# Offsets inside the weight buffers of the 512-column products, and a head written in a fixed order

## The chip, the cores and the metric

One core of a Trainium2 chip runs the program. TensorE (PE) multiplies matrices, VectorE (DVE), ScalarE (ACT) and GpSimd (POOL) work on elements, and SyncE (SP) and POOL issue transfers between the chip's memory and SBUF. The metric is the time of one execution on the device, in microseconds; the median of several runs counts.

## The reference, cut to what matters

One layer of an encoder on x (256 tokens of 2048 numbers, float32), with 16 learned tokens (`meta`) put in front, so T = 272.

```python
n      = rms_norm(h, norm_mix)                 # h: 272 x 2048
p      = n @ w_in                              # 14*512 mixing columns and 4*2048 gate columns
z      = [rglru(...), hyena(...), retention(...), hgrn2(...)]     # four mixers, each 272 x 512
up     = einsum('btnw,nwd->btnd', z, w_branch_out)
merged = sum over n of sigmoid(gate_cols) * up
h      = h + merged @ w_out
n      = rms_norm(h, norm_ffn)
h      = h + (silu(n @ w_gate) * (n @ w_up)) @ w_down             # 5632 hidden columns
out    = rms_norm(h, norm_final)               # the 256 tokens without meta
```

## The kernel before, in words

All weights come through one queue (SP) in pieces of 512 KB, `raw`, 128 partitions of 1024 numbers, in four buffers (`piece`). Each piece is split into two parts that TensorE multiplies in its fp32r format: `hi`, a cast (ACT, L112), and `lo` = raw − hi (DVE, L113). The first `NPOOL` = 2 pieces are split on POOL (L110, L113). `hi` and `lo` have three buffers each, of 1024 + `WPAD` = 1088 numbers, 4352 bytes, a multiple of 256; `piece` has a parameter `skip`, the number of elements by which the piece lies further in its buffer. The activations are split in the same way, and a product is three matmuls: hi by hi, lo by hi, hi by lo.

There are two kinds of product. In `mix_chunk` (L312 to L314) the weights are the stationary operand, 128 by 128, and the normalized tokens `nh`, `nl` move past: 272 columns (first token `t0` = 0), 258 (14) or 256 (16), each k of them a row of 320 numbers with 48 free ones (`LEAD`) in front. Here `skip` is 16 where `t0` isn't 0. In `xs_gemm` (L134 to L136) it is the other way round: tokens are stationary, and 512 columns of weights move past. It is used for the gates (stationary `nh`, 1536 matmuls), the up product of the mixers (`zh`, 384), the output product (`mth`, 384), the gate and up products of the feed-forward (`n2h`, 1056 each), and its down product in two parts (`hidh`, 576 and 480). Here `skip` isn't given and is 0. The last 120 matmuls of the down product take weights from separate buffers, `held`.

The head of the program loads `par` (constants), `xm` (meta tokens) and two tiles of 128 tokens of x, in halves of 512 KB. POOL issues `mlp` and `rope` before it does anything else. Each tile's squares are summed on ACT (L244) and DVE (L246) by quarters, a reciprocal root is made (L248, L161 to L163), and the tile is scaled by quarters on ACT (L255) and DVE (L257). Then, for each of 16 k, TensorE transposes 128 by 128 of both tiles (L280, `ptn`), ACT writes `nh` (L281) and DVE `nl` (L282). A scheduler decides the order on each engine; pieces are given a priority 250 steps ahead, and `SCHED` lists the order in which the mixers ask for chunks. Late in the mixing stage, `mixer_d` makes heads in `po` (L679 to L681), normalizes them in `head_out` into `on` (squares L499, root L161 to L163, scaling L509), transposes them (L512, `pt`) and multiplies them into `zz`; its gates are sigmoids `sg` (L520) and `fb` (L551), `bm` (L570) belongs to the decay.

## Time and profile before

| what | value |
|---|---|
| median of 3 runs | 1707.37 us (1707.24 to 1707.54) |
| the profiled execution's own time | 1708.65 us |
| its span, first to last instruction | 1706.9 us |
| TensorE busy | 1667.4 us, 98% |
| weight loads of TensorE | 1437.0 us, 84% |
| DVE, ACT, POOL busy | 954.6, 803.8, 80.6 us |
| mean granted clock of TensorE | 0.996 of full speed |
| moved by DMA | 313.81 MB, mean 184 GB/s |

Busy time is the time in which an engine executes instructions; weight loads run beside matmuls. A clock of 0.996 is a mean: 1.00 stands for 2.4 GHz and 0.50 for 1.2 GHz. The duration that the trace gives for one matmul includes a modelled end and is longer than the distance to the next, so lengths of matmuls are read from the distances of their starts.

### The profile page before, as it was taken

What the parts mean: (1) busy time and instruction counts of PE and PEld (TensorE: products, weight loads), DVE (VectorE), ACT (ScalarE), POOL (GpSimd) and SP (SyncE); (2) the same over time, 40 slices, a digit from 0 to 9 for tenths busy, and PEclk for the clock granted to TensorE, in tenths of its full rate; (3) what the DMA queues carried; (4) which work ended last, traced back from release to release, by engine and by line L of the source; (5) the groups of instructions that cost most, each with busy time, mean ns of one, the idle gap of its engine ahead of it and who ended that gap; (6) DMA issues with size and microseconds to landing.
All of it is one profiled execution on the core that took longest, in us unless ns stands there. A gap on an engine that the chain in (4) does not pass through costs nothing.

```text
span 1706.9 us, 22379 instructions
## 1 busy us (share of the span) xinstructions
PE 1667.4 (98%) x8844; PEld 1437.0 (84%) x8844; DVE 954.6 (56%) x1140; ACT 803.8 (47%) x969; POOL 80.6 (5%) x74
## 2 busy tenths in 40 slices
PE   6999999999999999999999999999999999999997
PEld 5999999989978888888888888888888888888886
DVE  6755895486675445454455545454545444544554
ACT  5544465474574444444445544444444334444443
POOL 2000000001002002010020000000000000000001
PEclk9999999999999999999999999999999999999999
DMA  6546444546356555555666555555555555555554
GB/s 238 184 140 193 144 140 145 181 139 212 111 172 211 188 194 186 196 194 188 197 198 210 197 197 186 192 190 187 191 190 188 194 196 190 194 185 190 193 191 142
DMA packets 87225, 313.81 MB, mean 184 GB/s; under 512 B 9824, under 2 KB 10112, under 8 KB 86992
## 3 DMA queue, kind: packets, MB, share of 16 engines
q1 hardware_dynamic: 84960, 304.42, 54.0%
q0 software_dynamic: 2160, 7.97, 1.5%
q8 instruction: 69, 1.13, 0.3%
q14 instruction: 36, 0.29, 0.1%
HBM read 309.17 MB, written 2.10 MB: 182 GB/s over the span
## 4 chain that ended last, share of the span: by engine, by line
PE 93%; DVE 4%; ACT 2%; issue 1%; DMA 0%; SPq 0%; ACTq 0%
PE acc L135 23%; PE acc L136 23%; PE acc L134 23%; PE mix L312 5%; PE mix L314 5%; PE mix L313 5%; DVE lo L113 1%; PE pth L948 1%; PE last L1006 1%; PE last L1005 1%; PE last L1007 1%; DMA x<-in_x_dram 0%; ACT hi L112 0%; PE pl L635 0%; PE pg L801 0%
## 5 line engine op out<-in xcount | busy, mean ns | idle before, releaser
L113 DVE TENSOR_TENSOR lo<-raw,hi 128x1024 fp32r<-128x1024 f32 x556 | 686.5, 1235 | 668.9 <-ACT hi L112 668.6
L112 ACT CAST hi<-raw 128x1024 fp32r<-128x1024 f32 x556 | 585.0, 1053 | 759.9 <-PE acc L136 620.1
L136 PE MATMUL acc<-hi,n2l 128*128 128x512 f32 x704 | 274.0, 389 | 0.0
L135 PE MATMUL acc<-lo,n2h 128*128 128x512 f32 x704 | 273.9, 389 | 0.0
L312 PE MATMUL mix<-nh,hi 128*128 128x272 f32 (+2 forms) x896 | 255.0, 287 | 3.4 <-DVE cg L521 1.8
L314 PE MATMUL mix<-nh,lo 128*128 128x272 f32 (+2 forms) x896 | 252.8, 287 | 4.3 <-DVE lo L113 4.3
L313 PE MATMUL mix<-nl,hi 128*128 128x272 f32 (+2 forms) x896 | 255.9, 287 | 0.0
L134 PE MATMUL acc<-hi,n2h 128*128 128x512 f32 x704 | 249.4, 390 | 0.0
L135 PE MATMUL acc<-lo,nh 128*128 128x512 f32 x512 | 200.1, 391 | 2.8 <-DVE lo L113 2.8
L136 PE MATMUL acc<-hi,nl 128*128 128x512 f32 x512 | 199.8, 390 | 0.0
L134 PE MATMUL acc<-hi,nh 128*128 128x512 f32 x512 | 181.7, 391 | 0.6 <-ACT hi L112 0.6
L312 PEld LDWEIGHTS mix<-nh,hi 128*128 128x128 f32 x896 | 169.9, 190 | 5.9 <-issue 2.8
L314 PEld LDWEIGHTS mix<-nh,lo 128*128 128x128 f32 x896 | 168.6, 190 | 6.1 <-DVE lo L113 5.2
L313 PEld LDWEIGHTS mix<-nl,hi 128*128 128x128 f32 x896 | 170.2, 190 | 0.7 <-issue 0.2
L136 PEld LDWEIGHTS acc<-hi,n2l 128*128 128x128 f32 x704 | 132.1, 188 | 27.5
L134 PEld LDWEIGHTS acc<-hi,n2h 128*128 128x128 f32 x704 | 132.2, 188 | 27.1
L135 PEld LDWEIGHTS acc<-lo,n2h 128*128 128x128 f32 x704 | 132.2, 188 | 27.1
L136 PE MATMUL acc<-hi,hidl 128*128 128x512 f32 x312 | 121.4, 389 | 0.0
L135 PE MATMUL acc<-lo,hidh 128*128 128x512 f32 x312 | 121.4, 389 | 0.0
L135 PEld LDWEIGHTS acc<-lo,nh 128*128 128x128 f32 x512 | 96.1, 188 | 24.0 <-DVE lo L113 4.5
L134 PEld LDWEIGHTS acc<-hi,nh 128*128 128x128 f32 x512 | 96.0, 188 | 20.9 <-ACT hi L112 1.3
L136 PEld LDWEIGHTS acc<-hi,nl 128*128 128x128 f32 x512 | 96.2, 188 | 19.6
(388 smaller groups left out, 1644.7 us busy)
## 6 DMA issues: line engine op xcount, KB each, us to landing
raw<-in_w_dram SPq DMA_DIRECT2D x568, 512.0 KB, 3.3
x<-in_x_dram SPq DMA_DIRECT2D x4, 512.0 KB, 8.7
h<-in_x_dram SPq DMA_DIRECT2D x8, 256.0 KB, 4.2
out_dram<-h SPq DMA_DIRECT2D x8, 256.0 KB, 3.1
lruw<-in_lruw_dram POOLq DMA_DIRECT2D x2, 512.0 KB, 6.3
dm<-in_decay_dram POOLq DMA_DIRECT2D x4, 256.0 KB, 4.3
nf<-in_norm_final_dram POOLq DMA_DIRECT2D x1, 1024.0 KB, 6.6
rot<-ck POOLq DMA_DIRECT2D x2, 272.0 KB, 6.0
```

What stands on the lines that cost most here:

```text
L112: A.copy(hi, raw)
L113: ins = (G if i < NPOOL else V).tensor_tensor(lo, raw, hi.bitcast(F32), op=SUB)
L134: PE.matmul(acc[t], xh[:, k, s], wh[:, j], start=(i + j == 0), stop=False)
L135: PE.matmul(acc[t], xh[:, k, s], wl[:, j], start=False, stop=False)
L136: PE.matmul(acc[t], xl[:, k, s], wh[:, j], start=False, stop=(i + j == n - 1))
L312: PE.matmul(o, wh[:, j, s], nh[:, k, t0:T], start=(k == 0), stop=False)
L313: PE.matmul(o, wh[:, j, s], nl[:, k, t0:T], start=False, stop=False)
L314: PE.matmul(o, wl[:, j, s], nh[:, k, t0:T], start=False, stop=(k == KT - 1))
L948: PE.transpose(pt[:, j * P:j * P + P], s[:, j * P:j * P + P], ident)
L1005: PE.matmul(acc, xh, wh, start=(k == 0), stop=False)
L1006: PE.matmul(acc, xh, wl, start=False, stop=False)
L1007: PE.matmul(acc, xl, wh, start=False, stop=(k == 2 * n - 1))
```

## The change

`xs_gemm` gets a parameter `skip` and hands it to `piece`. Every call gives a value of its own: gate 16 elements (64 bytes), up 4 (16 bytes), output 32 (128), feed-forward gate 48 (192), feed-forward up 56 (224), down 24 and 8 (96 and 32). The head is written in a fixed order: `par` comes in two transfers, the second behind x; `mlp` and `rope` are issued later on POOL; 40 transposes of `ident` (`pwarm`) are put ahead of those of x; the squares of both tiles come first, with one reciprocal root for both; then the scaling goes by quarters, tile 0 on ACT and tile 1 on DVE, between the steps over k; POOL splits its two pieces by quarters; and the first three pieces of ACT and DVE are held behind `nh` and `nl` of k = 5, 9 and 13.

```diff
--- before.py
+++ after.py
@@ -31,6 +31,7 @@
 NPOOL = 2
+NWARM = 40
@@ -83,13 +84,21 @@
         return psp.tile(list(shape), F32, tag="ps", name=name)
     par = const.tile([P, NPAR], F32, name="par")
-    nc.sync.dma_start(par, a["par"])
+    nc.sync.dma_start(par[:, :PCOL["norm_ffn"]], a["par"][:, :PCOL["norm_ffn"]])
     def pc(name, i=0, rows=P):
         return par[:rows, PCOL[name] + i:PCOL[name] + i + 1]
     ident = const.tile([P, P], F32, name="ident")
     make_identity(nc, ident)
+
+    last = {}
+    behind = {}
+
+    def after(ins, prev):
+
+        tc.add_manual_dep(ins.ins, prev.ins.name, mybir.DependencyInfo(
+            mybir.DependencyClass.NoSync, mybir.DependencyReason.DATA), reason="order at the head")
     wpos = [0]
     first = []
@@ -107,17 +116,26 @@
                 hi, lo = [p.tile([P, 1024 + WPAD], F32R, tag=x, name=x)[:, skip:skip + 1024]
                           .rearrange("p (k n) -> p k n", k=kt) for p, x in ((hip, "hi"), (lop, "lo"))]
             if i < NPOOL:
-                G.tensor_scalar(hi, raw, 1.0, 0.0, op0=MUL, op1=ADD)
+                for j in range(kt):
+                    ins = G.tensor_scalar(hi[:, j], raw[:, j], 1.0, 0.0, op0=MUL, op1=ADD)
+                    if "G" in last:
+                        after(ins, last["G"])
+                    ins = G.tensor_tensor(lo[:, j], raw[:, j], hi[:, j].bitcast(F32), op=SUB)
+                    last["G"] = ins
             else:
-                A.copy(hi, raw)
-            ins = (G if i < NPOOL else V).tensor_tensor(lo, raw, hi.bitcast(F32), op=SUB)
+                ins = A.copy(hi, raw)
+                if i in behind:
+                    after(ins, behind[i][0])
+                ins = V.tensor_tensor(lo, raw, hi.bitcast(F32), op=SUB)
+                if i in behind:
+                    after(ins, behind[i][1])
             if i == 1:
                 first.append(ins.ins)
         return hi, lo
     later = []
-    def xs_gemm(xh, xl, kts, at=2):
+    def xs_gemm(xh, xl, kts, at=2, skip=0):
 
         acc = [accp.tile([P, 512], F32, tag="acc", name=f"acc{t}") for t in range(2)]
@@ -126,7 +144,7 @@
             if i == at:
                 while later:
                     later.pop(0)()
-            wh, wl = piece(2, 512)
+            wh, wl = piece(2, 512, skip=skip)
             for j in range(2):
                 k = kts[i + j]
                 for t in range(2):
@@ -193,7 +211,6 @@
 
     mlp = H("mlp", 128 + T, rows=64)
-    G.dma_start(mlp, a["mlp"])
     f2 = mc.tile([P, T], F32, name="f2")
     def sine(dst, src, bias):
@@ -208,6 +225,7 @@
         A.activation(dst, x, AF.Sin)
     def sines():
+        G.dma_start(mlp, a["mlp"])
         p1 = ps("pf1")
         PE.matmul(p1[:64, :T], mlp[:33, 0:64], mlp[:33, 128:], start=True, stop=True)
         f1 = TT("f1", T, rows=64)
@@ -230,42 +248,20 @@
         for i in range(2):
             nc.sync.dma_start(halves[i], a["x"][t * P:t * P + P, i * 1024:i * 1024 + 1024])
         xts.append(halves)
+    nc.sync.dma_start(par[:, PCOL["norm_ffn"]:], a["par"][:, PCOL["norm_ffn"]:])
     ss = tiny("ss", 3, 4)
     rs = tiny("rs", 3)
     def quarter(g, q):
         return xts[g][q // 2][:, q % 2 * 512:q % 2 * 512 + 512]
...
     dump = H("dump", 256)
     A.activation(dump, xm, AF.Square, accum_out=ss[:, 2, 0:1])
     pm = ps("pmeta")
     PE.matmul(pm[:, 0:1], par[:, PCOL["ind"]:PCOL["ind"] + P], ss[:, 2, 0:1], start=True, stop=True)
     rsqrt(rs[:, 2:3], pm[:, 0:1], 1.0 / D)
-    squares(0, "AVAV")
-    squares(1, "AVAV")
     V.tensor_scalar(xm, xm, rs[:, 2:3], None, op0=MUL)
-    rescale(0, "AVAV")
-    rescale(1, "VAVA")
     pm = ps("pmeta")
     for b in range(2):
         PE.transpose(pm[:, b * P:b * P + P], xm[:, b * P:b * P + P], ident)
@@ -273,7 +269,41 @@
     gain = par[:, PCOL["norm_mix"]:PCOL["norm_mix"] + KT].rearrange("p (k b) -> p k b", b=2)
     V.tensor_tensor(nm, pm[:, 0:256].rearrange("p (b t k) -> p k b t", b=2, k=8),
                     gain[:, :, :, None].to_broadcast([P, 8, 2, META]), op=MUL)
-    split(nh[:, :, 0:META], nl[:, :, 0:META], nm.rearrange("p k b t -> p (k b) t"))
+    nm = nm.rearrange("p k b t -> p (k b) t")
+    last["A"] = A.copy(nh[:, :, 0:META], nm)
+    last["V"] = V.tensor_sub(nl[:, :, 0:META], nm, nh[:, :, 0:META].bitcast(F32))
+
+
+    pw_ = ps("pwarm")
+    for i in range(NWARM):
+        PE.transpose(pw_[:, i % 4 * P:i % 4 * P + P], ident, ident)
+
+
+    for t in range(2):
+        for q, e in enumerate("AVAV"):
+            dump = H("dump", 512)
+            x, acc = quarter(t, q), ss[:, t, q:q + 1]
+            if e == "A":
+                ins = A.activation(dump, x, AF.Square, accum_out=acc)
+            else:
+                ins = V.scalar_tensor_tensor(dump, x, 1.0, x, op0=MUL, op1=MUL, accum_out=acc)
+            after(ins, last[e])
+            last[e] = ins
+    V.tensor_reduce(rs[:, 0:2], ss[:, 0:2], op=ADD, axis=mybir.AxisListType.X)
+    rsqrt(rs[:, 0:2], rs[:, 0:2], 1.0 / D)
+
+
+    def rescale(q):
+        for t in range(2):
+            x, r = quarter(t, q), rs[:, t:t + 1]
+            if t == 0:
+                ins = A.activation(x, x, AF.Copy, scale=r)
+            else:
+                ins = V.tensor_scalar(x, x, r, None, op0=MUL)
+            after(ins, last["AV"[t]])
+            last["AV"[t]] = ins
+
+    rescale(0)
     for k in range(KT):
         pt = ps("ptn")
         for t in range(2):
@@ -281,6 +311,13 @@
         anchor = [A.activation(nh[:, k, META:], pt[:, :SEQ], AF.Copy, scale=pc("norm_mix", k)),
                   V.scalar_tensor_tensor(nl[:, k, META:], pt[:, :SEQ], pc("norm_mix", k), nh[:, k, META:].bitcast(F32),
                                          op0=MUL, op1=SUB)]
+        for e, ins in zip("AV", anchor):
+            after(ins, last[e])
+            last[e] = ins
+        if k % 4 == 1:
+            if k < 12:
+                rescale(k // 4 + 1)
+            behind[NPOOL + k // 4 - 1] = anchor
     def late(eng, ins):
         tc.add_manual_dep(ins.ins, anchor[eng].ins.name, mybir.DependencyInfo(
@@ -685,7 +722,8 @@
     def mixer_c():
         rope = H("rope", 2, T)
-        G.dma_start(rope, a["rope"])
+        with tc.issue_after(first[0]):
+            G.dma_start(rope, a["rope"])
         def rotate(x, n):
             y = S("rot", NW, n)
@@ -840,7 +878,7 @@
     nsh, nsl = nh[:, :, META:], nl[:, :, META:]
     def gate(d, b, first=False):
-        acc = xs_gemm(nsh, nsl, range(KT))
+        acc = xs_gemm(nsh, nsl, range(KT), skip=16)
         for t in range(2):
             s = half("sig")
             lut(s, acc[t], AF.Sigmoid, new=first and t == 0)
@@ -868,7 +906,7 @@
     def up(d):
         mg = [mgp.tile([P, 512], F32, tag="mg", name="mg") for _ in range(2)]
         for i, b in enumerate(BORDER):
-            acc = xs_gemm(zh[b], zl[b], range(NW))
+            acc = xs_gemm(zh[b], zl[b], range(NW), skip=4)
             for t in range(2):
                 s = sigs.pop((d, b, t))
                 if i == 0:
@@ -908,7 +946,7 @@
         rsqrt(rstd[:, i], rstd[:, i], 1.0 / D)
     for d in range(4):
-        acc = xs_gemm(mth, mtl, range(KT))
+        acc = xs_gemm(mth, mtl, range(KT), skip=32)
         for t in range(2):
             h = half("h")
             hh[t, d] = h
@@ -939,8 +977,8 @@
     hidl = [hid_p.tile([P, 4 * n, SEQ], F32R, tag=f"hid{i}l", name=f"hidl{i}") for i, n in enumerate(GU_HALF)]
     def gate_up(part, c):
-        ag = xs_gemm(n2h, n2l, range(KT), at=4)
-        au = xs_gemm(n2h, n2l, range(KT))
+        ag = xs_gemm(n2h, n2l, range(KT), at=4, skip=48)
+        au = xs_gemm(n2h, n2l, range(KT), skip=56)
         def turn(t, s):
             pt = ps("pth")
@@ -963,7 +1001,7 @@
     def down(part, ds):
         for d in ds:
-            acc = xs_gemm(hidh[part], hidl[part], range(4 * GU_HALF[part]))
+            acc = xs_gemm(hidh[part], hidl[part], range(4 * GU_HALF[part]), skip=8 if part else 24)
             for t in range(2):
                 add(acc[t], t, d, part == 1)
 
```

On POOL, at the head: the pieces of the two first weights, and the transfers `mlp`, `rope`. Before:

```order
L196 DMA mlp<-in_mlp_dram 64x400
L688 DMA rope<-in_rope_dram 128x544
masks.py:199 ISA
masks.py:199 AFFINE_SELECT ident<-ident 128x128
L110 TENSOR_SCALAR hi<-raw 128x1024
L113 TENSOR_TENSOR lo<-raw,hi 128x1024
```

After:

```order
masks.py:199 AFFINE_SELECT ident<-ident 128x128
L120 TENSOR_SCALAR hi<-raw 128x256
L123 TENSOR_TENSOR lo<-raw,hi 128x256
L120 TENSOR_SCALAR hi<-raw 128x256
...
L123 TENSOR_TENSOR lo<-raw,hi 128x256
L228 DMA mlp<-in_mlp_dram 64x400
L236 MEMSET f_98 64x272
L418 DMA trow<-in_trow_dram 128x31
L726 DMA rope<-in_rope_dram 128x544
```

The two transfers moved behind eight pairs of quarter pieces. On TensorE at the head (`x_0_...` are the first halves of the two token tiles, `mix_...` the two PSUM banks of the first chunk), before:

```order
L271 MATMUL pmeta<-ident,xm 128x128 x2
L280 MATMUL ptn<-ident,x_0_105 128x128 x4
L280 MATMUL ptn<-ident,x_0_109 128x128 x4
L312 MATMUL mix_261<-nh,hi 128x272
L312 MATMUL mix_262<-nh,hi 128x272
L280 MATMUL ptn<-ident,x_0_105 128x128
L280 MATMUL ptn<-ident,x_0_109 128x128
```

After:

```order
L267 MATMUL pmeta<-ident,xm 128x128 x2
L279 MATMUL pwarm<-ident 128x128 x40
L310 MATMUL ptn<-ident,x_0_104 128x128
L310 MATMUL ptn<-ident,x_0_108 128x128
...
L349 MATMUL mix_298<-nh,hi 128x272
L349 MATMUL mix_299<-nh,hi 128x272
L350 MATMUL mix_298<-nl,hi 128x272
L351 MATMUL mix_298<-nh,lo 128x272
L350 MATMUL mix_299<-nl,hi 128x272
```

The four transposes of either tile stood together and now alternate, behind the new ones. On ACT at the end of the first `mixer_d`, before:

```order
L499 ACTIVATE on_2564,ssh<-po 128x128 x4
L112 CAST hi<-raw 128x1024
L570 ACT_TABLE_LOAD
L570 ACTIVATE bm<-ff 128x32
L162 ACT_TABLE_LOAD
L162 ACTIVATE rsh<-rsh 128x4
L520 ACT_TABLE_LOAD
L520 ACTIVATE sg<-mix_2973 128x256
L112 CAST hi<-raw 128x1024
L520 ACTIVATE sg<-mix_2974 128x256
L551 ACTIVATE fb<-mix_2846 128x256
L551 ACTIVATE fb<-mix_2847 128x256
```

After:

```order
L536 ACTIVATE on_2614,ssh<-po 128x128 x4
L607 ACT_TABLE_LOAD
L607 ACTIVATE bm<-ff 128x32
L180 ACT_TABLE_LOAD
L180 ACTIVATE rsh<-rsh 128x4
L126 CAST hi<-raw 128x1024 x2
L588 ACT_TABLE_LOAD
L588 ACTIVATE fb<-mix_2896 128x256
L588 ACTIVATE fb<-mix_2897 128x256
L174 CAST zh_286<-zz 128x512
L557 ACTIVATE sg<-mix_3023 128x256
```

One `hi` stood ahead of the root (L162, after the change L180) and now stands behind it, and `fb` stood behind two `sg` and now comes ahead of them. On TensorE at the same place, before, where 34 mixing matmuls stand between the last `po` and `pt`:

```order
L314 MATMUL mix_2973<-nh,lo 128x256
L312 MATMUL mix_2974<-nh,hi 128x256
L313 MATMUL mix_2974<-nl,hi 128x256
L314 MATMUL mix_2974<-nh,lo 128x256
L512 MATMUL pt<-ident,on_2564 128x128 x4
L312 MATMUL mix_3102<-nh,hi 128x272
L313 MATMUL mix_3102<-nl,hi 128x272
L314 MATMUL mix_3102<-nh,lo 128x272
L312 MATMUL mix_3102<-nh,hi 128x272
```

After, where 40 stand between the last `po` and the first `pt`:

```order
L349 MATMUL mix_3024<-nh,hi 128x256
L350 MATMUL mix_3024<-nl,hi 128x256
L549 MATMUL pt<-ident,on_2614 128x128
L351 MATMUL mix_3024<-nh,lo 128x256
L349 MATMUL mix_3023<-nh,hi 128x256
L549 MATMUL pt<-ident,on_2614 128x128
L350 MATMUL mix_3023<-nl,hi 128x256
L549 MATMUL pt<-ident,on_2614 128x128
L351 MATMUL mix_3023<-nh,lo 128x256
L349 MATMUL mix_3024<-nh,hi 128x256
L549 MATMUL pt<-ident,on_2614 128x128
L350 MATMUL mix_3024<-nl,hi 128x256
```

The four `pt` stood together behind the last matmul of their chunk and now stand among its matmuls; 20 more of that chunk follow the last of them.

## Rows read from the trace of the kernel before

**Rows 1.** The page: busy us, share of the span, instructions.

```profile
PE 1667.4 (98%) x8844; PEld 1437.0 (84%) x8844; DVE 954.6 (56%) x1140; ACT 803.8 (47%) x969; POOL 80.6 (5%) x74
```

**Rows 2.** TensorE's waits, the longest group: us in total, times, longest.

```profile
PE pmeta L271 <- DVE xm L266: 4.7, 1, 4.7
```

**Rows 3.** Timeline, 512-column products: start, duration, ... (first and last of 179 matmuls).

```profile
1349.65 0.39 PE L135 MATMUL acc<-lo,hidh 128*128 128x512 f32 x1
...
1390.00 0.39 PE L135 MATMUL acc<-lo,hidh 128*128 128x512 f32 x1
```

**Rows 4.** Timeline, mixing: pairs of first and last, 95, 191 and 96 matmuls.

```profile
108.61 0.29 PE L312 MATMUL mix<-nh,hi 128*128 128x272 f32 x1
...
120.21 0.28 PE L313 MATMUL mix<-nl,hi 128*128 128x272 f32 x1
...
120.46 0.28 PE L312 MATMUL mix<-nh,hi 128*128 128x256 f32 x1
...
142.01 0.28 PE L313 MATMUL mix<-nl,hi 128*128 128x256 f32 x1
...
164.86 0.28 PE L314 MATMUL mix<-nh,lo 128*128 128x256 f32 x1
...
176.26 0.28 PE L313 MATMUL mix<-nl,hi 128*128 128x258 f32 x1
```

**Rows 5.** Timeline at the head: six matmuls over the first two rows.

```profile
21.76 0.43 PE L312 MATMUL mix<-nh,hi 128*128 128x272 f32 x1
...
22.90 0.43 PE L314 MATMUL mix<-nh,lo 128*128 128x272 f32 x1
...
24.15 0.29 PE L314 MATMUL mix<-nh,lo 128*128 128x272 f32 x1
```

**Rows 6.** Timeline of the head, all engines.

```profile
12.52 0.88 DVE L257 TENSOR_SCALAR x<-x,rs 128x512 f32<-128x512 f32 x2
...
13.29 1.12 PE L280 MATMUL ptn<-ident,x 128*128 128x128 f32 x4 [2.84 <-ACT x L255]
...
13.93 0.69 DVE L246 SCALAR_TENSOR_TENSOR dump<-x 128x512 f32<-128x512 f32 x1
...
14.23 1.29 POOL L110 TENSOR_SCALAR hi<-raw 128x1024 fp32r<-128x1024 f32 x1 [11.31 <-DMA raw<-in_w_dram]
...
15.11 0.16 DVE L248 TENSOR_REDUCE rs<-ss 128x1 f32<-128x4 f32 x1 [0.49 <-ACT dump L244]
...
15.60 2.34 POOL L113 TENSOR_TENSOR lo<-raw,hi 128x1024 fp32r<-128x1024 f32 x1
...
15.93 3.48 DVE L257 TENSOR_SCALAR x<-x,rs 128x512 f32<-128x512 f32 x2
...
18.28 1.12 PE L280 MATMUL ptn<-ident,x 128*128 128x128 f32 x4 [3.87 <-DVE x L257]
...
19.41 0.79 PE L312 MATMUL mix<-nh,hi 128*128 128x272 f32 x2
```

**Rows 7.** Windows: stretch, length, TensorE busy (instructions), clock, DMA share, GB/s.

```profile
10.00:12.00 2.00, 0.45 (x2) 1.00 1.03 420
```

**Rows 8.** Windows, the same columns, in the mixing stage.

```profile
276.60:283.40 6.80, 5.46 (x23) 0.50 0.26 77
```

**Rows 9.** Timeline around the end of the first mixer_d.

```profile
270.32 0.28 ACT L499 ACTIVATE on<-po 128x128 f32<-128x128 f32 x1 [3.40 <-PE po L681]
...
271.39 1.05 ACT L112 CAST hi<-raw 128x1024 fp32r<-128x1024 f32 x1
...
274.01 0.28 PE L314 MATMUL mix<-nh,lo 128*128 128x256 f32 x1
...
275.29 0.20 ACT L162 ACTIVATE rsh<-rsh 128x4 f32<-128x4 f32 x1
...
276.14 1.25 PE L512 MATMUL pt<-ident,on 128*128 128x128 f32 x4 [1.85 <-DVE on L509]
...
278.73 0.59 PE L312 MATMUL mix<-nh,hi 128*128 128x272 f32 x1 [1.34 <-ACT fb L551]
```

More of the change, by code (lines that the diff above doesn't have):

```diff
@@ L59 @@
 _n = 0
-for _name, _w in (("norm_mix", 16), ("norm_ffn", 16), ("lcw", 16), ("lcb", 4), ("lba", 8), ("lbx", 8), ("lam", 8),
+for _name, _w in (("norm_mix", 16), ("ind", P), ("norm_ffn", 16), ("lcw", 16), ("lcb", 4), ("lba", 8), ("lbx", 8), ("lam", 8),
                   ("hcw", 36), ("hcb", 12), ("hbias", 4), ("lb", 4), ("b1", 1), ("b2", 1), ("dec", 8),
-                  ("negt", 2), ("nyq", 1), ("ind", P), ("fill", 48)):
+                  ("negt", 2), ("nyq", 1), ("fill", 48)):
     PCOL[_name] = _n
@@ L237, in quarter @@
         return xts[g][q // 2][:, q % 2 * 512:q % 2 * 512 + 512]
-    def squares(g, engs):
-        for q, e in enumerate(engs):
-            dump = H("dump", 512)
-            x, acc = quarter(g, q), ss[:, g, q:q + 1]
-            if e == "A":
-                A.activation(dump, x, AF.Square, accum_out=acc)
-            else:
-                V.scalar_tensor_tensor(dump, x, 1.0, x, op0=MUL, op1=MUL, accum_out=acc)
-        r = rs[:, g:g + 1]
-        V.tensor_reduce(r, ss[:, g], op=ADD, axis=mybir.AxisListType.X)
-        rsqrt(r, r, 1.0 / D)
-    def rescale(g, engs):
-        for q, e in enumerate(engs):
-            x, r = quarter(g, q), rs[:, g:g + 1]
-            if e == "A":
-                A.activation(x, x, AF.Copy, scale=r)
-            else:
-                V.tensor_scalar(x, x, r, None, op0=MUL)
     dump = H("dump", 256)
```

## The prediction

> **What bounds the kernel now.** I read the page first: TensorE is busy for 1667.4 of 1706.9 us, 98%, and no other engine for more than 56% [rows 1]. So a change can pay in two ways only: by shortening what TensorE waits for, or by shortening its matmuls. The list of TensorE's waits shows that the first is small: the longest group of them sums to 4.7 us, at the very start [rows 2]. The second is large. The start times of long runs of matmuls give the step from one to the next: (1390.00 − 1349.65)/178 = 226.7 ns for 512 columns [rows 3], (142.01 − 120.46)/190 = 113.4 ns for 256, (120.21 − 108.61)/94 = 123.4 ns for 272, and (176.26 − 164.86)/95 = 120.0 ns for 258 [rows 4]. There are 5472 products of 512 columns, so they hold 5472 × 0.2267 = 1240 us, nearly three quarters of the time. The reader is to see two things. The matmuls run without a gap, whatever DVE and ACT do beside them. And 512 and 256 columns cost the same per column, 0.4428 and 0.4430 ns, against 1/2.4 = 0.4167 ns for a column per cycle of the granted upper clock: a loss of one part in sixteen that every such matmul has.
>
> **The offsets.** All tiles begin at multiples of 256 bytes, so today each 512-column moving operand begins at 0 within 256 bytes, and so does its stationary operand. The 256-column chunks are the one other case at hand: their stationary operand (the weights, `skip=16`) begins 64 bytes in, their moving one (`nh` from column 64 of its pitch) at 0. Both pay the same 17/16. So the relation of the two operands does not set this loss as far as the rows go, and I take the offsets of the 5352 shifted products (5472 less the 120 in `held`) at nothing. DVE and ACT write the shifted buffers; should that cost them a few per cent, it is covered: they are busy 56% and 47% of the span [rows 1], and TensorE would be late only if one of them came near its own share.
> The ends. Downwards: if an offset lifts the loss wholly, a step falls from 226.7 to 213.3 ns, 13.4 × 5352 = 71.6 us. What speaks for such a loss by the clash of two streams is that it is gone at half clock: five steps of 272 columns take 22.90 − 21.76 = 1.14 us, 228 ns each, and 272/1.2 is 226.7 [rows 5]. A stream that is delayed by memory would look like that; a limit on what one stream is given would too, and no offset would lift it.
> Upwards: the two forms whose moving operand does not begin on a 256-byte boundary are the two that cost more than 17/16. The 272-column one begins at 192 and takes 3.0 ns over its 120.4; the 258-column one begins at 248 and takes 5.8 over its 114.2 [rows 4]. After the change all shifted moving operands begin off the boundary, at 16 to 224 bytes. By 3.0 ns each that is +16.1 us, by 5.8 ns +31.0 us. If it is only one boundary more to cross (4 cycles in each 64 columns are lost now, so 4/2.4 = 1.67 ns), it is +8.9 us. Against it: neither column count is a multiple of 64, so the excess can come from the ragged end as well. I stay at zero, with −71.6 and +31 as ends.
>
> **The head.** Before, the scaling of the second token tile waits three times over. Its transfer comes behind `par`, `mlp` and `rope` (0.16, 0.10 and 0.28 MB by their shapes); its squares stand on ACT and DVE behind the scaling of the first tile; and the scaling itself (two of L257) takes 3.48 us from 15.93, against 0.88 for the first tile's two, while POOL runs a 2.34 us subtraction from 15.60 [rows 6]. So the first mixing matmul starts at 19.41 [rows 6].
> After, 0.10 + 0.28 + 0.09 MB leave the road ahead of x. At 420 GB/s [rows 7] that is 1.1 us: the last half of x lands at about 11.8 instead of my estimate of 12.9 (it was there by 13.93, where DVE squares it, and the first piece of weights, a transfer behind it, by 14.23 [rows 6]). Squares 0.69 (L246), one chain of reduce, ACT and reciprocal 15.93 − 15.11 = 0.82, then one quarter's scaling to the transpose 13.29 − 12.52 = 0.77, transposes and `nh` to the first matmul 19.41 − 18.28 = 1.13 [rows 6]: 11.8 + 3.4 = 15.2, which is 4.2 us earlier. DVE can then be held by one quarter of a POOL subtraction at a time (2.34/4 = 0.6 us and a little fixed cost), not by a whole one. From there POOL paces the first eight k: a pair takes at least (1.29 + 2.34)/4 = 0.9 us, at most perhaps 1.2; TensorE needs 6 × 0.123 + 2 × 0.108 = 0.96 us a k at full clock and nearly twice that at half. So POOL costs at most some 0.3 us. `mlp` is issued behind POOL's last piece, near 22.3 (14.23 − 1.1 + 8 × 1.15); I can't read whether its matmul will wait for it and put 0 to 0.5 us into the ends.
> The clock. Before, the steps are at half speed until about 24.0 (durations of 0.43 until 22.90, 0.29 from 24.15 [rows 5]), 4.6 us after the mixing begins at 19.41. In the other place with a fall, mixing resumes at 278.73 and the half clock lasts until 283.4, 4.7 us [rows 8, 9]. In both, transposes ran shortly ahead, from 18.28 and from 276.14, and the lags agree when counted from the matmuls (4.6 and 4.7), not when counted from the transposes (5.7 and 7.3). So I expect the 40 new transposes of `pwarm` not to bring the rise forward: gain 4.2 us. If they do, the 4.6 us at half speed go as well, 2.3 us, together −6.5.
> The Trainium skill bears on this (TensorE: Matmul & The Clock Gate, Part 4: PE-mode transpose): the clock gate's upper state does not engage for transposes. By that rule the head is worth the 4.2 us; without it 6.5. The two lags agree with it. By that rule the sum below is 1697, without it 1695.
> Value for the head −4.2, ends −3.3 and −6.5.
>
> **The region at 274 to 283 us.** The scheduler moves instructions at the end of `mixer_d(0)` (the order in the part on the change). Before: the last 256-column matmul starts at 274.01; then the four transposes `pt` wait until 276.14 for `on`, whose chain runs squares, one `hi` cast of 1.05 us, a table load, `bm`, a table load, the square root at 275.29, `on`; then L312 waits until 278.73 for `fb` (its bank of PSUM), which stands behind `sg`, a `hi` cast and `sg`; and the idle stretch drops the clock to half until 283.4 [rows 8, 9]. The price: 276.14 − 274.13 = 2.0 idle; from the last transpose near 277.0 to 278.73 idle, 1.7; the mixing of 283.4 − 278.73 = 4.7 us at half speed, half of which is lost, 2.35; the transposes at half speed 0.3. Sum 6.4 us.
> After, the `hi` cast is behind the square root, so the chain from the last `po` to `on` is 1.05 shorter: 270.32 to 276.14 is 5.8 before, 4.8 after. 40 mixing matmuls instead of 34 stand between `po` and the first `pt`, 40 × 0.1134 = 4.5 us, and a further 25 stand among and behind the `pt`. `fb` comes behind its table load, ahead of `zh` and `sg`, though two `hi` casts still stand before it: 274.4 + 2 × 1.05 + 1.28 (a table load by the rows before) + 0.66 = 278.4. The bank is wanted after all 65 matmuls and four `pt`, near 270.1 + 7.4 + 0.5 = 278.0. So 0.4 us of waiting is left and the clock stays up: −6.0, ends −2.0 (only the order on ACT helps, the clock still falls) and −6.4.
>
> **Sum.** 1708.65 (the profiled execution: span 1706.9 and 1.75 around it) − 4.2 − 6.0 + 0 = 1698.45. That execution lies 1.28 above the median of 1707.37, so 1697.2 as a median: 1697.
>
> **The rivals.**
> Off the boundary costs (ends on the other side). Mechanism: every shifted 512-column moving operand begins inside a 256-byte block, as the 272- and 258-column ones do. Price 1.67 to 3.0 ns × 5352 = 8.9 to 16.1 us, against −10.2 from the rest: 1706 to 1713. Above 10.2/5352 = 1.9 ns a matmul the kernel is slower than before. For it: the two forms off the boundary are exactly the two above 17/16. Against: both have ragged column counts.
> The offsets lift the loss. Mechanism: the moving stream meets the weight loads or the writes of ACT and DVE at the same place within 256 bytes, and moves out of their way. A quarter of the bound, 18 us, gives 1679; the whole gives 1626. For it: no loss at half clock. Against it: the 256-column chunks, already in another relation, pay the same; and the loss grows with the columns, not with the number of weight loads.
> A page of the Trainium skill gives another size for that bound (TensorE: Matmul & The Clock Gate, Wait — 56ns, not 53.3ns?): 215.7 ns for 512 warm columns, a fixed 2.5 ns over the cycles. By it 11.0 × 5352 = 59 us would be to be had, an estimate. The rows here differ: 13.4 ns are lost on 512 columns and 6.7 on 256, so here it is not a fixed amount.
> The moved instructions do not help (the waits only shift, the clock falls anyway): the head alone, −4.2, or the region alone, −6.0, gives 1701 to 1703.
>
> **How the numbers follow.** Offsets neutral and both stretches pay, 38%, own range 1693 to 1700. Cost, 30%: half of it within 0.2% (3.4 us, about what a measurement can tell from no change), nearly all the other half slower. Lifted loss, 27%, from a few us to much more. One stretch fails, 5%, mostly still faster. So faster 38 + 27 + 4 + 1 = 70%, same 15%, slower 15%. The range runs from 1676 (leaving out a gain of over 21 us by the offsets, about 13 in 100) to 1713 (leaving out a cost over 3.0 ns, about 6).
>
> **What would show it.** The step of 512 columns in each stage, gate 64, up 16, output 128, feed-forward gate 192 and up 224, down 96 and 32 bytes in: 226.7 in all if I am right; 228 to 230 by the first rival; under 226 in some kinds by the second. The first `mix` matmul near 15.2 and half-speed steps until about 19.9. No half clock near 277, and no wait over 0.6 us for `on` or `fb`. I am wrong above all if one kind's step moves by more than 2 ns.

## The result

The changed kernel takes 1724.53 us (median of 4 runs, 1723.32 to 1724.91) against 1707.3 us before. The ratio is 1.010, with a 95% interval of 1.0083 to 1.0118: slower by 17 us, where 10 us faster were forecast, and outside the range.

The page of the changed kernel, engines' busy time, and the chain that ended last:

```profile
PE 1696.6 (98%) x8884; PEld 1439.7 (84%) x8884; DVE 951.7 (55%) x1137; ACT 799.6 (46%) x968; POOL 81.9 (5%) x86
...
PE 93%; DVE 3%; ACT 2%; issue 1%; POOL 0%; DMA 0%; SPq 0%; ACTq 0%
```

TensorE is busy for 29 us longer [rows 1], with 40 more instructions. No new wait explains that. The timeline of TensorE in a gate product (offset 64 bytes) and in a feed-forward up product (224 bytes), each from the first to the last of 96 matmuls:

```profile
562.09 0.62 PE L152 MATMUL acc<-hi,nh 128*128 128x512 f32 x2
...
583.83 0.39 PE L154 MATMUL acc<-hi,nl 128*128 128x512 f32 x1
...
988.49 0.63 PE L152 MATMUL acc<-hi,n2h 128*128 128x512 f32 x2
...
1010.64 0.40 PE L154 MATMUL acc<-hi,n2l 128*128 128x512 f32 x1
```

21.74/95 = 228.8 ns and 22.15/95 = 233.2 ns, against 226.7 [rows 3]. Read in this way, as the mean distance between starts with stalls left out, the stages of the changed kernel against the kernel before are:

| product | offset, bytes | matmuls | step before, ns | step after, ns | us together |
|---|---|---|---|---|---|
| gate | 64 | 1536 | 227.0 | 229.0 | 3.1 |
| up | 16 | 384 | 226.7 | 231.7 | 1.9 |
| output | 128 | 384 | 227.0 | 232.9 | 2.3 |
| feed-forward gate | 192 | 1056 | 226.8 | 233.3 | 6.9 |
| feed-forward up | 224 | 1056 | 226.7 | 233.3 | 7.0 |
| down, part 0 | 96 | 576 | 226.7 | 233.4 | 3.9 |
| down, part 1 | 32 | 360 | 226.7 | 233.4 | 2.4 |
| `held` | none | 120 | 226.7 | 227.1 | 0 |

The sum is 27.5 us. The rest of the change did pay. At the head, the timeline (its columns as in [rows 6]):

```profile
6.27 6.48 PE L279 MATMUL pwarm<-ident 128*128 128x128 f32 x40
12.83 1.09 PE L310 MATMUL ptn<-ident,x 128*128 128x128 f32 x8
13.92 0.49 PE L349 MATMUL mix<-nh,hi 128*128 128x272 f32 x2
...
18.90 0.39 PE L351 MATMUL mix<-nh,lo 128*128 128x272 f32 x1 [0.29 <-POOL lo L123]
...
20.93 0.39 PE L351 MATMUL mix<-nh,lo 128*128 128x272 f32 x1 [1.01 <-POOL lo L123]
```

The first mixing matmul starts at 13.92 instead of 19.41 [rows 6], and two waits for POOL's quarters are new. At the end of the first `mixer_d`, the timeline of TensorE, and the windows over it:

```profile
266.45 0.33 PE L549 MATMUL pt<-ident,on 128*128 128x128 f32 x1 [0.18 <-DVE on L546]
...
269.85 0.29 PE L349 MATMUL mix<-nh,hi 128*128 128x272 f32 x1
```

```profile
266.00:270.00 4.00, 3.82 (x34) 1.00 0.17 44
270.00:274.00 4.00, 4.00 (x35) 1.00 0.73 231
```

The two waits of 1.85 and 1.34 us [rows 9] have become one of 0.18, and the clock, which stood at 0.50 here for 6.8 us [rows 8], stays at 1.00.

### The profile page after: what moved, and what is told of

Same layout as the page of the kernel before. It is cut to its first block, busy times and chain, and to the rows that moved or that the text cites. A ratio compares the mean times of both kernels' runs of the same rounds, so it can differ in the third digit from the quotient of the medians.

```text
span 1723.1 us, 22476 instructions
## 1 busy us (share of the span) xinstructions
PE 1696.6 (98%) x8884; PEld 1439.7 (84%) x8884; DVE 951.7 (55%) x1137; ACT 799.6 (46%) x968; POOL 81.9 (5%) x86
## 4 chain that ended last, share of the span: by engine, by line
PE 93%; DVE 3%; ACT 2%; issue 1%; POOL 0%; DMA 0%; SPq 0%; ACTq 0%
PE acc L153 24%; PE acc L154 24%; PE acc L152 24%; PE mix L351 5%; PE mix L349 5%; PE mix L350 5%; DVE lo L129 1%; PE pth L986 1%; PE last L1045 1%; PE last L1044 1%; PE last L1043 1%; DMA raw<-in_w_dram 0%; ACT hi L126 0%; PE pl L672 0%; PE pg L839 0%
## 5 line engine op out<-in xcount | busy, mean ns | idle before, releaser
L154 PE MATMUL acc<-hi,n2l 128*128 128x512 f32 x704 | 278.1, 395 | 0.0
L153 PE MATMUL acc<-lo,n2h 128*128 128x512 f32 x704 | 278.0, 395 | 0.0
L152 PE MATMUL acc<-hi,n2h 128*128 128x512 f32 x704 | 253.5, 396 | 0.0
L154 PE MATMUL acc<-hi,hidl 128*128 128x512 f32 x312 | 123.7, 397 | 0.0
L153 PE MATMUL acc<-lo,hidh 128*128 128x512 f32 x312 | 123.3, 395 | 0.0
```

The costliest lines, as they stand in the source:

```text
L152: PE.matmul(acc[t], xh[:, k, s], wh[:, j], start=(i + j == 0), stop=False)
L153: PE.matmul(acc[t], xh[:, k, s], wl[:, j], start=False, stop=False)
L154: PE.matmul(acc[t], xl[:, k, s], wh[:, j], start=False, stop=(i + j == n - 1))
```

## The experiments

Two questions were open: whether the offsets alone cost the time, and by what. For the second there were three theories: the place of the moving operand within 256 bytes (the prediction's first rival), the writes of ACT and DVE into shifted buffers, and the distance between the two operands. Distance means here the start of the moving operand less that of the stationary one, within 256 bytes, so 0 to 255. The starts follow from the sizes of the tiles: in the built programs `hi`, `lo`, `nh`, `nl`, `n2h`, `mth` and `hidh` lie on multiples of 256 bytes, before a `skip` or the columns in front are added; the traces show no addresses. All kernels but the last two keep the order of instructions of the changed kernel or of the one before.

**1. The head without the offsets.** `skip` is 0 in all calls of `xs_gemm`:

```diff
-        acc = xs_gemm(nsh, nsl, range(KT), skip=16)
+        acc = xs_gemm(nsh, nsl, range(KT), skip=0)
...
```

> The changed kernel with every offset back at 0. Theory (the offsets cost it all): in the changed kernel the step of 512 columns is 229.0 ns in the gates and 231.7 to 233.4 in the other shifted products, against 226.7; over 1536 and 3816 matmuls that is 27.4 us, so this kernel should take 1724.5 - 27 = 1697, with 226.7 ns in every stage. Rival (something in the new head or in the moved order disturbs TensorE's stream later): the steps stay at 229 to 233 without the offsets, and the time near 1724.

Measured: 1698.56 us (1698.0 to 1698.67), ratio 0.9946 to before, interval 0.9929 to 0.9962. The step is 226.7 to 227.0 ns in every stage. The offsets cost 1724.5 − 1698.6 = 26 us, and the rest of the change gains 9.6. It is a version that beats both kernels.

**2. The offsets without the head**, the kernel before with the same seven values:

```diff
-            wh, wl = piece(2, 512)
+            wh, wl = piece(2, 512, skip=skip)
...
```

> The kernel before with the offsets of the change alone, nothing else moved. Theory: 1707.3 + 27 = 1734.7, the same steps per stage as in the changed kernel, and the waits of before at the head and at 274 to 283. Rival (the cost belongs to the head and the order): 1707.

Measured: 1734.55 us (1733.46 to 1735.36), ratio 1.0156, interval 1.0141 to 1.0171, with the steps of the table above in every stage. So the two parts add up, and the offsets are the whole of the loss. 27.5 us by steps stand against 26.0 and 26.4 by times; where the remaining 1.3 us went was not followed.

**3. One offset for all, 16 elements.** All seven values are 16.

> The changed kernel with one offset, 16 elements (64 bytes), for all products of 512 columns. The gates had this offset and paid 2.3 ns a matmul, all others 5 to 6.7. Theory that the start within 256 bytes alone sets the price: every stage 228 to 230 ns, 1697 + 5352 x 2.2 = 1709. Rival, the price belongs to the stationary operand that stands beside it (nh has rows of 1280 bytes, n2h, mth and hidh of 1024): gates 229, the others 232 to 233 as they are, 1724.

Measured: 1708.88 us (1708.19 to 1709.84), ratio 1.0006, interval 0.9997 to 1.0016. The steps are 228.9 to 229.0 in all seven stages. The feed-forward up product, first and last of 96 matmuls:

```profile
985.49 0.62 PE L152 MATMUL acc<-hi,n2h 128*128 128x512 f32 x2
...
1007.23 0.39 PE L154 MATMUL acc<-hi,n2l 128*128 128x512 f32 x1
```

21.74/95 = 228.8: it pays what the gates pay. The kind of product does not matter, the offset does.

**4. One offset for all, 64 elements, a whole block of 256 bytes.**

> The changed kernel with an offset of 64 elements (256 bytes) for all: shifted, but on the boundary of 256 bytes again. Theory (the place within 256 bytes counts): 226.7 ns in every stage, 1697. Rival (any shift of the buffers costs, because hi and lo no longer lie as before among the other tiles): 229 to 233 ns, about 1724.

Measured: 1698.19 us (1697.99 to 1698.57), ratio 0.9944, interval 0.9929 to 0.9959, 226.7 to 227.0 ns in every stage. Shifting as such costs nothing. Up to here the place within 256 bytes and the distance within 256 bytes say the same, since all stationary operands of these products begin on a boundary.

**5. Only `lo` shifted, by 48 elements.**

```diff
-                hi, lo = [p.tile([P, 1024 + WPAD], F32R, tag=x, name=x)[:, skip:skip + 1024]
-                          .rearrange("p (k n) -> p k n", k=kt) for p, x in ((hip, "hi"), (lop, "lo"))]
+                hi, lo = [p.tile([P, 1024 + WPAD], F32R, tag=x, name=x)[:, s0:s0 + 1024]
+                          .rearrange("p (k n) -> p k n", k=kt) for p, x, s0 in ((hip, "hi", skip if kt == 4 else 0), (lop, "lo", skip))]
```

> Offset 48 elements (192 bytes) for lo alone in every 512-column product; hi stays at 0. Theory (TensorE pays for reading an operand that begins inside a block of 256 bytes): of the three matmuls of a product only the one that moves lo gets longer, by 6.6 ns, the two that move hi stay at 226.7; 5352/3 x 6.6 = 11.8 us, so 1698.5 + 11.8 = 1710. Rival (the shifted writes of DVE get in the way of TensorE's reads, whatever it reads): all three forms get longer alike, by a third of 6.6 or more.

Measured: 1718.38 us (1717.73 to 1718.72), ratio 1.0062, interval 1.0048 to 1.0075; the mean step is 230.4 to 230.6 in all stages. The extra time doesn't stay with the matmul that moves `lo`: it goes round over all three forms, in a pattern that repeats after twelve matmuls (226 to 236 ns), with means of 232.1 (hi by hi), 231.5 (the one that moves `lo`) and 227.8. The theory's 11.8 us were too few against 19.8 measured, so a price per matmul by its own operand is refuted. The rival, DVE's writes, had all three longer alike, which they are not. The trace of the changed kernel speaks against it too: in the feed-forward gate and up products, 134 steps during which ACT, DVE and POOL all stood idle took 234.0 ns in the mean, and 1505 steps wholly beside their work 233.2. Its last 22 shifted matmuls (1683.78 to 1688.68 us) keep 233.4 though ACT and DVE write only into `held` by then, which has no offset. So the extra time of a matmul does not need a write at a shifted place beside it.

**6. The stationary operand shifted.** `n2h` and `n2l` begin 192 bytes further in; their gate product moves weights 192 bytes in, their up product weights at 0.

```diff
-    n2h = np_.tile([P, KT, SEQ], F32R, tag="nh", name="n2h")
...
+    n2h, n2l = [np_.tile([P, KT * SEQ + 48], F32R, tag=x, name="n2" + x[1])[:, 48:].rearrange("p (k n) -> p k n", k=KT)
+                for x in ("nh", "nl")]
```

> The normalized tokens of the feed-forward (n2h and n2l, stationary) begin 192 bytes further; its gate product moves weights 192 bytes in as well, its up product weights at 0. Theory (the place of the moving operand alone): gate 233.3 ns, up 226.7 ns. Rival (the distance between stationary and moving operand): gate 226.7, up 233. The time is 1705.5 by both; the steps decide.

Measured: 1701.74 us, one run. TensorE in a gate product (the first two rows) and the up product behind it:

```profile
1403.28 0.62 PE L152 MATMUL acc<-hi,n2h 128*128 128x512 f32 x2
...
1424.83 0.39 PE L154 MATMUL acc<-hi,n2l 128*128 128x512 f32 x1
...
1425.05 0.63 PE L152 MATMUL acc<-hi,n2h 128*128 128x512 f32 x2
...
1446.81 0.39 PE L154 MATMUL acc<-hi,n2l 128*128 128x512 f32 x1
```

21.55/95 = 226.8 with both shifted, 21.76/95 = 229.1 with the stationary operand alone. The moving operand of the first begins 192 bytes into its block and pays nothing: the theory of its place is refuted, the prediction's first rival with it. The second pays 2.4 ns though its moving operand lies on the boundary. The expected 233 was wrong in the sign of the distance: 0 − 192 is 64 within 256 bytes, and 2.2 ns is the price of 64 (experiment 3).

**7. Seven other offsets, one for each kind.**

```diff
-        acc = xs_gemm(nsh, nsl, range(KT), skip=16)
+        acc = xs_gemm(nsh, nsl, range(KT), skip=2)
...
```

> Seven other offsets, one for each kind of product, since the price was the same for all kinds at 64 bytes: gates 8 bytes, up 48, output 80, feed-forward gate 160, feed-forward up 240, down 112 and 176. Theory A (any place off the boundary costs about one sum, 5 to 7 ns, and 64 bytes is an exception for a reason of its own): 231.5 to 233.5 in all seven. Theory B (the price falls smoothly towards 64 bytes): 48 and 80 bytes lie between 229 and 231.5, the others at 232 to 233.5. By A 1698.5 + 5352 x 6 = 1731, by B about 1728.

Measured: 1728.66 us, one run. In bytes: 8, 233.6 ns; 48, 233.3; 80, 231.1; 112, 231.1; 160, 234.2; 176, 231.2; 240, 231.2. Neither theory: no smooth fall to 64, and not one sum for all.

The 231.2 of 240 bytes is no step that any matmul has. The eleven feed-forward up products of this run take 226.7 and 236.3 to 236.6 ns in turn. Two of them, first and last of 96:

```profile
995.67 0.62 PE L152 MATMUL acc<-hi,n2h 128*128 128x512 f32 x2
...
1017.21 0.39 PE L154 MATMUL acc<-hi,n2l 128*128 128x512 f32 x1
...
1040.80 0.63 PE L152 MATMUL acc<-hi,n2h 128*128 128x512 f32 x2
...
1063.28 0.40 PE L154 MATMUL acc<-hi,n2l 128*128 128x512 f32 x1
```

21.54/95 = 226.7 and 22.48/95 = 236.6, with the same operands at the same distance. The kernel before does it as well: its 256-column chunks run at 113.4 ns in most stretches and at 117.8 in others, without a gap and with nothing moved:

```profile
339.71 0.28 PE L312 MATMUL mix<-nh,hi 128*128 128x256 f32 x1
...
350.49 0.28 PE L314 MATMUL mix<-nh,lo 128*128 128x256 f32 x1
...
494.60 0.40 PE L314 MATMUL mix<-nh,lo 128*128 128x256 f32 x2
...
505.32 0.28 PE L314 MATMUL mix<-nh,lo 128*128 128x256 f32 x1
```

Those are 10.78/95 = 113.5 and 10.72/91 = 117.8. So a distance can have two steady steps. What picks one of them was not followed.

**8. The free columns behind the rows.** No offsets; all of `nh` and `nl` begin 192 bytes earlier in their rows, which is 64 bytes on within 256.

```diff
-    nh, nl = [np_.tile([P, KT, LEAD + T], F32R, tag=x, name=x)[:, :, LEAD:] for x in ("nh", "nl")]
+    nh, nl = [np_.tile([P, KT, LEAD + T], F32R, tag=x, name=x)[:, :, :T] for x in ("nh", "nl")]
```

> No offsets; the 48 free columns of nh and nl lie behind a row instead of in front, so that the 272-column operands begin on a boundary of 256 bytes, the 256-column ones 64 bytes in and the 258-column ones 56 bytes in. Theory (the start sets the price): 272 columns take 120.4 ns instead of 123.4, 256 columns 113.4 + 1.1 = 114.5, 258 about 117; 1344 x 3.0 - 1152 x 1.1 + 192 x 3 = 3.3 us less, 1695.2. Rival (the ragged end of 272 and 258 columns costs, not the start): 123.4, 113.4 and 120.0 as they are, 1698.5.

Measured: 1713.73 us (1712.63 to 1714.82), ratio 1.0035, interval 1.0021 to 1.0049. Neither answer: 272 columns, now on the boundary, take 125.4 ns instead of 123.4 to 123.7, 256 columns 119.7 instead of 114.5. In the gates the stationary operand is now 64 bytes in and the weights are at 0. TensorE in one of them:

```profile
568.97 0.63 PE L152 MATMUL acc<-hi,nh 128*128 128x512 f32 x2
...
591.13 0.40 PE L154 MATMUL acc<-hi,nl 128*128 128x512 f32 x1
```

22.16/95 = 233.3. The distance is 0 − 64, which is 192, and 233.3 is the price of 192 in the table of the result. In the mixing chunks the distance was 192 for 272 and 256 columns and is 0 now: there 192 is the good place and 0 the dear one, the reverse of 512 columns.

**9. The same, with the weights moved along**, so that every distance is as before and every place another:

```diff
-            wh, wl = piece(4, 256, skip=16 if t0 else 0)
+            wh, wl = piece(4, 256, skip=32 if t0 else 16)
...
-        acc = xs_gemm(nsh, nsl, range(KT), skip=0)
+        acc = xs_gemm(nsh, nsl, range(KT), skip=16)
```

> The free columns behind the rows of nh and nl again, which moves all these operands by 64 bytes, and now the weights beside them moved by 64 bytes too (gates offset 16 elements, mixing chunks 16 and 32 instead of 0 and 16). Theory (TensorE's price goes by the distance between the moving operand and the stationary one within 256 bytes, not by where either begins): every distance is as in the kernel before, so gates 226.7, 272 columns 123.4, 256 columns 114.4, time 1698.5. Rival (the place of an operand itself counts): gates 229 (moving operand 64 bytes in, as with the single offset), 256 columns 119.7 as with the free columns behind alone, about 1710.

Measured: 1698.35 us (1698.0 to 1698.64), ratio 0.9946, interval 0.9933 to 0.996. The gates:

```profile
561.63 0.62 PE L152 MATMUL acc<-hi,nh 128*128 128x512 f32 x2
...
583.16 0.39 PE L154 MATMUL acc<-hi,nl 128*128 128x512 f32 x1
```

21.53/95 = 226.6; 272 columns take 123.5, 256 columns 115.1. Here ACT and DVE write every gate's and every mixing chunk's weights to shifted places and the moving operands begin off the boundary, and the time is that of experiment 1. The distance of the writes to the stationary operand is kept here as well, but the steps without such writes, under experiment 5, speak against them. That leaves the distance between the moving and the stationary operand, as what decides whether a stream can run at its best step.

**10. A map of distances in one run.** Each gate product, feed-forward gate product and mixing chunk has its own offset, from a list:

```diff
+GATEMAP = list(range(0, 64, 4))
+FFMAP = [1, 2, 3, 5, 6, 7, 10, 13, 18, 30, 63]
...
```

> A map in one run, no other change: each of the 16 gate products of 96 matmuls gets its own offset, 0 to 240 bytes in steps of 16; the 11 feed-forward gate products get 1, 2, 3, 5, 6, 7, 10, 13, 18, 30 and 63 elements; the 14 chunks of 272 columns get 0 to 208 bytes in steps of 16 for their stationary weights, the 12 chunks of 256 columns 0 to 240. Theory (distance of the two operands, the kernel before lies at the best place): no place under 226.7 ns for 512 columns, and none under 123.4 and 113.4 for 272 and 256; the largest near 234. Rival (there are places that lift the loss of one part in sixteen): some under 224.

Measured: 1719.89 us, one run. Mean step, stalls left out, 96 matmuls each:

```
gate, bytes   0  16  32  48  64  80  96 112 128 144 160 176 192 208 224 240
ns          227.7 231.7 233.1 233.2 229.1 231.0 233.4 231.1 232.5 233.3 234.2 233.4 233.3 234.6 233.3 226.7
ff gate, elements 1   2   3   5   6   7  10  13  18  30  63
ns          237.7 233.6 229.0 239.0 233.5 227.3 233.4 233.4 235.4 234.2 228.0
```

The gate at 0 runs among the mixing, hence 227.7. No place is under 226.7. For 272 columns the weights at 0 (in the other runs) and 32 bytes give 123.4, the other places 125.1 to 126.7; for 256 columns none of the twelve places tried reached the 113.4 that 64 bytes mostly give (mean 114.5): they give 117.3 to 119.9. So the kernel before lies at the best distances found in all three forms; for 272 columns 160 is as good as its 192. Two values differ from experiment 7: 240 bytes take 226.7 in a gate here, the lower of the two steps there; 176 bytes take 233.4 here and 231.1 to 231.4 in the down products there, which stays open. As most places were tried in one product only, a place that has two steps shows one of them here.

**11. One warm-up transpose instead of 40.**

```diff
-NWARM = 40
+NWARM = 1
```

The scheduler moves a few matmuls at the head and near `mixer_d` with it.

> No offsets, and one new transpose (pwarm) instead of 40. With 40 the steps of the transposes fell from 213 to 109 ns after 14 of them, 3.0 us from the first; mixing then ran at full clock from its start. Theory (those transposes bring the rise forward): half speed from 13 until 17 to 19 us, 3 to 4.6 us of mixing of which half is lost, 1.5 to 2.3, less what TensorE now waits for POOL at this place (1.7): 1699 to 1700.5. Rival (they do nothing, the clock would have risen anyway): 1698.5, steps of 123 ns from the first mixing matmul.

Measured: 1698.96 us (1698.6 to 1699.64), ratio 0.995, interval 0.9937 to 0.9964. The timeline of TensorE where its steps fall from 227 ns:

```profile
16.60 0.43 PE L350 MATMUL mix<-nl,hi 128*128 128x272 f32 x1
16.82 0.43 PE L351 MATMUL mix<-nh,lo 128*128 128x272 f32 x1
17.05 0.35 PE L350 MATMUL mix<-nl,hi 128*128 128x272 f32 x1
17.24 0.29 PE L351 MATMUL mix<-nh,lo 128*128 128x272 f32 x1
```

At 17.05 us the full clock is there, 4.0 us after the first transposes of x and 2.4 us after the first mixing matmul (14.64). With 40 of them (experiment 1), the windows of TensorE while nothing but these transposes ran:

```profile
6.70:9.60 2.90, 2.90 (x15) 1.00 1.03 414
9.70:12.40 2.70, 2.70 (x26) 1.00 1.04 418
```

2.9 us hold some 14 starts of 213 ns, the next 2.7 us some 25 of 109 ns: the full clock came 3.0 us after the first of the 40, with no other matmul in between. The clock column reads 1.00 in the first row too, because the trace holds no record of the clock before one of full clock at 9.69 us (17.18 in this experiment); the steps tell. So the transposes do raise the clock. But it pays little: 0.4 us between the medians of experiments 1 and 11, about their scatter. TensorE is faster at full clock and then waits for POOL's quarters: 0.7 us in experiment 1, nothing here.

Differences as small as this may have another source as well. In the traces of this experiment, of the changed kernel and of experiment 12 the clock is at half for another 3.4 us, from about 474 to 477 us on, where those of experiments 1 and 9 and of the kernel before have it full. The windows of TensorE there, here and in experiment 1:

```profile
474.60:477.90 3.30, 3.08 (x7) 0.50 0.51 159
474.60:477.90 3.30, 3.00 (x12) 1.00 0.47 159
```

**12. `mlp` and `rope` at the head of POOL's queue**, as before the change:

```diff
     mlp = H("mlp", 128 + T, rows=64)
+    G.dma_start(mlp, a["mlp"])
...
-        with tc.issue_after(first[0]):
-            G.dma_start(rope, a["rope"])
+        G.dma_start(rope, a["rope"])
```

Seven matmuls of the head change places with it.

> No offsets, and the transfers of mlp and rope at the head of POOL's queue as in the kernel before. Theory (0.38 MB ahead of x on the road): x and the first weights land 0.9 us later and everything behind them too, 1699.4, the first mixing matmul at 15.1 instead of 14.2. Rival (they pass beside x): 1698.5, 14.2.

Measured: 1700.0 us (1699.27 to 1701.45), ratio 0.9957, interval 0.9943 to 0.9971; 1.6 us above the 1698.35 of experiment 9, which ran on the same chip. The first mixing matmul starts at 15.22 instead of 14.19 in experiment 1:

```profile
15.22 0.49 PE L349 MATMUL mix<-nh,hi 128*128 128x272 f32 x2
```

## Why the prediction was wrong

**The offsets: the step that failed.** The prediction put the 5352 shifted products at nothing, from "the relation of the two operands does not set this loss as far as the rows go". They cost 26 us (experiments 1 and 2), 27.5 by steps. The relation is what sets it (experiments 6, 8 and 9), with some relations that have two steps (experiment 7). The inference went wrong where it took two forms with the same loss at two relations for one form that doesn't care: 512 columns have their good place at distance 0, 256 and 272 columns a good one at 192, and the kernel before had put each at its own. One row of each form could not show that; it would have needed one form at two distances, and the trace of before has none. It did have a warning: that all 256-column matmuls lose the same sixteenth was read from one stretch, and other stretches of the same form run at 117.8 ns.

**The upper end.** The range ended at 1713 because I priced the cost by the 272- and 258-column rows, 3.0 and 5.8 ns, and took the lower. The mean price is 27.5/5352 = 5.1 ns, near the other end that I had named: 1697 + 31.0 would have been 1728. The excess of the 272 columns [rows 4] does not come from their start: on the boundary they take 123.5 ns when the weights move along (experiment 9), and no distance tried took less than 123.3. Whether it is the ragged end was not tried.

**The rivals.** The first had the right sign by the wrong mechanism (the place of the moving operand; refuted by experiment 6, where an operand 192 bytes off the boundary pays nothing). The second came nearest, with two streams that meet at a place within 256 bytes, but had the wrong sign: at the distances tried, moving them apart made it worse. That they meet is argued from the distances; no trace shows it. Whether it is the operand loaded beside a matmul or its own one that counts was not told apart; the weight load of the next matmul runs while a matmul streams (PEld is busy 84% beside PE's 98%), so I would look there first. The loss of one part in sixteen at the best distance stays unexplained as well.

**The head.** Forecast −4.2, measured −5.2 up to the second stretch: the copy `vt`, the same instruction ahead of the second stretch, starts at 217.42 us before and at 212.18 in experiment 1. The start of the mixing was forecast for 15.2 and came at 13.9 to 14.2. That the transposes would not bring the clock's rise forward was wrong (experiment 11): the steps fell from 213 to 109 ns while nothing but transposes ran. With it falls here what the Trainium skill says (TensorE: Matmul & The Clock Gate, Part 4: PE-mode transpose), that the clock's upper state does not engage for transposes; the two equal lags of the trace before were too few to bear it. What the clock gave, POOL's pace took back: its quarters were to cost 0.3 us and cost 1.3 in waits alone (0.7 in experiment 1). `mlp` and `rope` were worth 0.9 us at the forecast's 420 GB/s, of its 1.1 with the second part of `par`; by the start of the mixing in experiment 12 they are worth 1.0, by its median 1.6.

**The region at 274 to 283.** Forecast −6.0, measured −5.4: from `vt` to the first gate matmul the kernel before takes 305.24 − 217.42 = 87.8 us, experiment 1 294.64 − 212.18 = 82.5. Rows of both kernels, before and experiment 1:

```profile
217.42 0.57 ACT L596 COPY vt<-pv 128x512 f32<-128x512 f32 x1
...
305.24 0.48 PE L134 MATMUL acc<-hi,nh 128*128 128x512 f32 x1
```

```profile
212.18 0.57 ACT L633 COPY vt<-pv 128x512 f32<-128x512 f32 x1
...
294.64 0.48 PE L152 MATMUL acc<-hi,nh 128*128 128x512 f32 x1
```

As forecast, `fb` is no longer waited for, `on` for 0.17 us only, and the clock doesn't fall. Together −10.6 in the profiled executions and −9.6 in the medians, against −10.2.

## What to carry to other kernels

Where TensorE is the bound, the distance between the starts of its moving and stationary operands within 256 bytes is a parameter of the time: some 5% of a 512-column fp32r matmul hung on it, and the best value differs by the number of columns. Price it by giving each call of one product another distance and reading the steps of all from one trace; then run the chosen distance in many products, and look at each of them, since a mean can hide two steps. A cost at a resource that is 98% busy is hardly covered: its unknown end belongs in the range whole.

## What the runs showed of the hardware

The step of a 512-column matmul of fp32r went from 226.7 to 239.0 ns with nothing changed in the product but the offset of its moving operand by 20 bytes (experiment 10), and back to 226.7 with an offset of 256 (experiment 4). The price isn't smooth: 12 and 28 bytes cost 2.3 and 0.6 ns, 4 and 20 bytes 11 and 12. At one distance a stream can run at either of two steady steps: 226.7 and 236.6 ns at 240 bytes (experiment 7), 113.4 and 117.8 for 256 columns in the kernel before. When only one of three matmuls of a product was shifted, all three got slower (experiment 5), so a delay in one may move the next against its weight load; that is argued from the pattern, not shown. And with nothing but 128 by 128 transposes against an identity on TensorE, its steps fell from 213 to 109 ns, from half to full clock, 3.0 us after the first of them.
